# Hybrid decoder layer: FFN input normed ahead of its products, 18 of 22 up pairs by seven block products, gated products through DRAM, the down projection as one stage, w_out weights kept

## The chip, the cores and the metric

The kernel runs on one core of one Trainium2 chip. The metric is the device time of one execution in microseconds (us). Shorter is better. TensorE (PE) multiplies; VectorE (DVE), ScalarE (ACT) and GpSimd (POOL) work element by element; SyncE (SP) and the queues of ACT and POOL start the transfers between DRAM and the on-chip memory.

## The reference

One decoder layer over 1024 prompt tokens and 32 sample tokens (8 sequences of 4), all in fp32. Cut to the half of the layer that the change touches:

```
merged = sum_i sigmoid(g_i) * (y_i @ W_branch_i)      # three token mixers, y_i
x   = x + rmsnorm(merged @ w_out) * g_post
up  = (rmsnorm(x) * g_pre_f) @ w_up                    # 1024 -> 2 * 2816
upc = causal_dwconv3(up) + b                           # over time, 3 taps a channel
fa, fb = split(upc)                                    # 2816 each
x   = x + rmsnorm((silu(fa) * fb) @ w_down) * g_post_f # 2816 -> 1024
```

The layer also returns its states: among them the last rows of the key and value caches (`out_wk`, `out_wv`: for the sample tokens the old cache less its first 4 rows, so a copy from DRAM to DRAM, with the new rows filled in elsewhere) and the last two values of `up` of each channel (`out_fx`).

## The kernel before

**Products.** The 1056 tokens stand in three chunks of 352 columns. Activations and weights are held as a high and a low part of a 32-bit format that PE multiplies, and a product of two numbers is three matmuls: high by high, high by low, low by high. A weight piece is four blocks of 128 by 128; it is loaded on SP's queue (L133) and split by `split`: ACT copies out the high part (L89, `wh`), DVE subtracts to get the low part (L95, `wl`). A ring of three pieces lies between the splitting and PE; `make` asks for pieces some places ahead. `products` multiplies one output tile of 128 channels: with k = 1024 it takes 8 blocks times 3 matmuls times 3 chunks, 72 matmuls of 352 columns. An up pair is two such tiles, `za` and `zb` of the same j, and there are 22 pairs (`w_up` as 44 tiles).

**Seven block products.** The ten pairs of gate tiles earlier in the program go through `strassen` instead: the pair is taken as a 2 by 2 block matrix (two tiles by two halves of k), the input as 2 by 2 blocks (two halves of k by two column halves of 264), and seven products of blocks stand for eight. That is 168 matmuls of 264 columns a pair. It needs sums of input blocks, made once by `combos` into the buffer Y, sums of weight blocks (four DVE additions a pair on 128 by 512), and sums of results: some results are written by ACT to their place, and others are added by DVE from the accumulators "mm", "aux" and "wb".

**Stages.** After the start (the norm of x, then gates of the first chunk), the gates and the mixers, the branch products end at 640.13 us. Then `w_out` is multiplied in three passes, one a chunk, each of which loads and splits all its weights again (24 units of 24 matmuls). After a chunk's pass, `chain` brings it on while PE works on the next one: sum of squares by a product with ones, root (`rstd_of`, `factor_of`: DVE L295, the power on POOL L296, spread by four transposes L301), times the factor, plus x loaded from DRAM, the sum written to `x2d`, squares, and another root into R. `operands` makes the FFN input x times `g_pre_f` without that root (L903, L904), in Y; the root, which is one factor a token, is multiplied in when an up result leaves its accumulator (`evac_u`, by DVE). So up products start before the second root is known. The last chunk's chain (`last_chain`) runs beside the up pairs j = 0 and 1.

**Up and down.** Then the pairs j = 2 to 21: two units, the convolution over time (`conv`: ACT L983, then DVE L985 twice a tile), silu (L1036), the product, and its split into high and low parts in a ring of five slots, from which `down` takes groups of four as soon as they are there: DOWN lists after which j which k are multiplied. M holds the down sums of all chunks. The last group and the final norm follow.

**Order.** PE's instructions run in the order in which the code makes them; those of the other engines are put in order by a scheduler at build time, so a line may be moved far from where it is written. SP issues nearly all loads.

Of the kernel before, what the change touches and what calls it, by code (L numbers as in the profile page):

```python
# [31 lines left out]
RING = 5  # L32
LAST = 18
DOWN = {4: [(0, 4)], 8: [(4, 8)], 12: [(8, 12)], 16: [(12, 16)], 21: [(16, 18)]}
# [5 lines left out]
def body(tc, i, o):  # L40
# [3 lines left out]
    with top, tc.manual_schedule(engines={mybir.EngineType.PE}):  # L44
# [15 lines left out]
        M8 = M.rearrange("p (k t) -> p k t", k=8)  # L60
        x2d = dram.tile([P, 8, T], F32, name="x2d")

# [57 lines left out]
        xraw = [None]  # L120
# [25 lines left out]
        def make(ahead):  # L146
            while len(made) < min(ahead, len(items)):
                need, _, fn = items[len(made)]
                load(need + 4)
                if len(raws) <= need:  # L150
                    break
                made.append(fn())

        def add(src, nk, eng, where=None):
            for k0 in range(0, nk, 4):
                n = min(4, nk - k0)
                w = None if where is None else [t[:, k0 : k0 + n, :] for t in where]
# [3 lines left out]
                def fn(at=at, n=n, w=w):  # L161
                    raw, raws[at] = raws[at], None
                    return split(raw, n, w, eng)
# [3 lines left out]
        def add_pair(one, two):  # L167
# [7 lines left out]
            def part(q):  # L175
                def fn():
# [6 lines left out]
                    if q == 6:  # L183
                        tt(raws[at + 1], raws[at + 1], raws[at], ALU.subtract)
# [9 lines left out]
        def products(nk, hi, lo, evac, chunks=CHUNKS, cols=cc, pieces=None):  # L194
            ps = {}
            for pi, k0 in enumerate(range(0, nk, 4)):
# [6 lines left out]
                else:  # L203
                    make(pieces + pi + (3 if pieces >= lastw else 1))
# [44 lines left out]
        def combos(X, to, p):  # L249
# [4 lines left out]
            to4 = lambda n, h: to[:, ((p * 4 + n) * 2 + h) * 4 * HC :][:, : 4 * HC].rearrange("p (k t) -> p k t", k=4)  # L254

            def part(n, z):
                copy(to4(n, 0), z)
                sub(to4(n, 1), z, f32(to4(n, 0)))
# [47 lines left out]
        hs = ExitStack()  # L306
        with hs:
            hp = open_pool(hs, "hp", bufs=1)
            H = hp.tile([P, 16, T], F32R, name="H")
            Hhi, Hlo = (lambda k: H[:, k, :]), (lambda k: H[:, 8 + k, :])  # L310
            win = lambda u: i["win"][u]


            sigd = dram.tile([P, 24, T], F32, name="sigd")
            Yf = Y.rearrange("p s t -> p (s t)")

            nc.scalar.dma_start(cst[:, :NC1], i["cst"][:, :NC1])
            dve.memset(nhalf, -0.5)
            dve.memset(ones, 1.0)
            warm = fixed.tile([P, 4], F32, name="warm")  # L320
            copy(warm, nhalf)
            make_identity(nc, ident)
            for u in range(3):
                add(win(16 + u), 8, dve, [Y[:, 8 + 2 * u + h, 0:1024].rearrange("p (k m) -> p k m", k=8) for h in range(2)])
            add(win(19), 8, dve)
            for u in range(20, 40, 2):
                add_pair(win(u), win(u + 1))
            for u in (0, 1, 2):
                add(win(u), 8, dve)
            for u in range(3, 16):  # L330
                add(win(u), 8, pool)
            for n in range(8):
                add(i["wa"][n], 2, dve)
                add(i["wc"][n], 2, dve)
                add(i["wb"][n], 4, dve)
            for c in CHUNKS:
                for n in range(8):
                    add(i["wo"][n], 8, dve)
            for eng in (dve, pool):
                for j in range(2):  # L340
                    for part in range(2):
                        add(i["wu"][j + NFF * part], 8, eng)
            for j in range(2, NFF):
                for part in range(2):
                    add(i["wu"][j + NFF * part], 8, dve)
                for g0, g1 in DOWN.get(j, ()):
                    for n in range(8):
                        add(i["wd"][n, :, g0:g1, :], g1 - g0, dve)
            lastw = len(items)
            for n in range(8):  # L350
                add(i["wd"][n, :, LAST:NFF, :], NFF - LAST, pool if n % 2 else dve,
                    [Y[:, 2 + n, 512 * h : 512 * (h + 1)].rearrange("p (k m) -> p k m", k=4) for h in range(2)])
            room[3] = R[:, 544:T]

            def load_x(c, k, n=2):
                nc.sync.dma_start(M8[:, k : k + n, cc(c)], i["x"][c, :, k : k + n, :])

            load(1)
            load_x(0, 0, 1)
            load_x(0, 1, 1)  # L360
            for k in (2, 4, 6):
                load_x(0, k)
            load(4)
            for c in (1, 2):
                for k in range(0, 8, 2):
                    load_x(c, k)

            with ExitStack() as gs:
                psW = open_pool(gs, "psW", bufs=2, space=PSUM)
                banks[:] = [(psA, "mm")] * 3 + [(psW, "wb")] * 2  # L370
                sg = open_pool(gs, "sg", bufs=1)

                def evac_gate(u):
                    def f(c, ps):
                        s = sg.tile([P, CW], F32, name="g", bufs=3)
# [21 lines left out]
                def end(c):  # L397
                    later[c]()
                    normed(c)
# [844 lines left out]
```

## Time and profile before

| | |
|---|---|
| median of 3 runs | 1554.22 us (1553.83 to 1555.48) |
| the profiled run's own time | 1555.17 us |
| its span in the profile | 1553.5 us |
| start, until the first product of the gates | 0 to 44.0 us |
| gate pairs by seven block products | 84.8 to 289.5 us |
| mixers and branch products | to 640.1 us |
| `w_out`, and up pairs 0 and 1 | 640.1 to 807.7 us |
| up pairs 2 to 21 with the down groups | 807.7 to 1483.2 us |
| last down group and final norm | 1483.2 to 1553.5 us |

The lines of such a profile are read as follows. A row on a group of instructions has the line, the engine, the operation, the written and the read buffers, the shape and the count; behind the first bar the busy time of all in us and the mean of one in ns; behind the second the idle time of that engine just before them, and what ended it. The chain of waits goes back from the last instruction to what released each step, and each of its rows has a start, a duration and the instruction. The windows list for a stretch its length, the busy time (and number of instructions) of PE, PE's weight loads, DVE, ACT and POOL, then PE's granted clock (1.00 is full), the mean share of the 16 DMA engines that was busy, and GB/s. A busy share of DMA just above 1 is a rounding of the profile and means full.

### The profile page before, as it was taken

Reading aid. Unit: us, or ns where it says so; the run is one execution under the profiler, and the core shown is the slowest. Engines: PE = TensorE matmul, PEld = TensorE weight load, DVE = VectorE, ACT = ScalarE, POOL = GpSimd, SP = SyncE. Lnnn points to the kernel's source line nnn. Section 1 sums busy time; section 2 is a strip of 40 time slices with the busy share of each in tenths; the row PEclk is TensorE's granted clock in tenths of the full one; section 3 lists DMA queues with packets and bytes.
Section 4 is the critical chain, followed back from the end, with each engine's and each line's share of the span. In section 5 each row is a group of like instructions: output and inputs, shape, how many; then the busy total and the mean of one; then the engine's idle time right before and its main releaser. Section 6 shows DMA issues by size and latency. Waiting matters only on the chain.

```text
span 1553.5 us, 24657 instructions
## 1 busy us (share of the span) xinstructions
PE 1491.7 (96%) x9707; PEld 1479.0 (95%) x9707; DVE 875.1 (56%) x1542; ACT 583.7 (38%) x1123; POOL 317.5 (20%) x378
## 2 busy tenths in 40 slices
PE   5899999999999999978999999999999999999995
PEld 5899999998999899978999999999999999999995
DVE  7744445237676366577766515653654555355757
ACT  6344444356764322445442332321321232132343
POOL 2100000023553045244571101100110010010024
PEclk9999999999999999999999999999999999999997
DMA  6123332210002176444531111111111111111225
GB/s 221 52 97 111 106 109 84 82 50 28 28 22 77 46 232 189 135 149 156 175 99 48 48 42 48 48 42 48 48 42 48 48 41 49 48 41 45 65 73 175
DMA packets 77187, 128.01 MB, mean 82 GB/s; under 512 B 8192, under 2 KB 34752, under 8 KB 77056
## 3 DMA queue, kind: packets, MB, share of 16 engines
q1 hardware_dynamic: 68896, 111.66, 22.8%
q10 hardware_dynamic: 8032, 13.41, 2.3%
q8 instruction: 76, 1.25, 0.3%
q0 software_dynamic: 144, 1.38, 0.2%
q14 instruction: 39, 0.32, 0.1%
HBM read 104.17 MB, written 23.26 MB: 82 GB/s over the span
## 4 chain that ended last, share of the span: by engine, by line
PE 88%; DVE 6%; POOL 2%; ACT 2%; issue 1%; DMA 1%; SPq 0%; POOLq 0%; ACTq 0%; DVEq 0%
PE mm L98 54%; PE mb L98 23%; PE aux L98 6%; PE wb L98 3%; DVE M L92 2%; POOL rs L296 1%; PE sp L98 1%; ACT M L673 1%; DVE Y L904 1%; PE aux L686 1%; DVE M L390 0%; POOL R L92 0%; DVE M L667 0%; DMA M<-in_x 0%; DVE wl L95 0%
## 5 line engine op out<-in xcount | busy, mean ns | idle before, releaser
L98 PE MATMUL mm<-Y,wh 128*128 128x352 f32 (+1 forms) x1984 | 453.8, 314 | 0.0
L89 ACT ACTIVATE wh<-raw 128x512 fp32r<-128x512 f32 (+1 forms) x242 | 147.0, 608 | 522.8 <-PE mm L98 213.2
L98 PEld LDWEIGHTS mm<-Y,wh 128*128 128x128 f32 x1984 | 337.5, 189 | 0.0
L98 PE MATMUL mm<-Y,wl 128*128 128x352 f32 (+1 forms) x992 | 312.0, 315 | 0.7 <-DVE wl L95 0.7
L98 PE MATMUL mm<-H,wh 128*128 128x352 f32 (+1 forms) x1184 | 282.4, 323 | 1.6 <-DVE Y L95 0.9
L98 PE MATMUL mb<-Y,wh 128*128 128x352 f32 x992 | 241.8, 325 | 0.0
L95 DVE TENSOR_TENSOR wl<-raw,wh 128x512 fp32r<-128x512 f32 (+1 forms) x208 | 154.2, 741 | 144.8 <-ACT wh L89 144.3
L98 PEld LDWEIGHTS mm<-H,wh 128*128 128x128 f32 x1184 | 203.9, 191 | 2.5 <-PE aux L98 1.1
L98 PE MATMUL mm<-H,wl 128*128 128x352 f32 (+1 forms) x592 | 189.7, 320 | 4.1 <-DVE wl L95 4.0
L98 PEld LDWEIGHTS mm<-Y,wl 128*128 128x128 f32 x992 | 186.1, 188 | 1.0 <-DVE wl L95 1.0
L98 PEld LDWEIGHTS mb<-Y,wh 128*128 128x128 f32 x992 | 174.1, 189 | 0.0
L98 PE MATMUL mb<-Y,wl 128*128 128x352 f32 x496 | 161.4, 325 | 0.0
L985 DVE SCALAR_TENSOR_TENSOR cz<-U,cst,cz 128x1072 f32<-128x1072 f32 x88 | 118.2, 1344 | 31.6 <-ACT cz L983 30.3
L98 PE MATMUL mm<-ring,wh 128*128 128x352 f32 x524 | 126.6, 323 | 0.0
L980 POOL COPY fx<-U 128x2 f32<-128x2 f32 x44 | 30.2, 687 | 460.7 <-DVE U L92 460.7
L98 PEld LDWEIGHTS mm<-H,wl 128*128 128x128 f32 x592 | 112.9, 191 | 5.1 <-DVE wl L95 5.1
L95 DVE TENSOR_TENSOR wl<-xraw,wh 128x512 fp32r<-128x512 f32 x70 | 48.5, 692 | 90.0 <-ACT wh L89 89.5
L98 PEld LDWEIGHTS mb<-Y,wl 128*128 128x128 f32 x496 | 93.4, 188 | 0.0
L98 PEld LDWEIGHTS mm<-ring,wh 128*128 128x128 f32 x524 | 91.6, 188 | 0.0
L92 DVE TENSOR_TENSOR U<-mm,R 128x352 f32<-128x352 f32 (+2 forms) x106 | 43.1, 428 | 80.7 <-PE mm L98 80.7
L92 DVE TENSOR_TENSOR M<-mm,M 128x352 f32<-128x352 f32 (+3 forms) x95 | 47.4, 505 | 70.8 <-PE mm L98 70.5
L98 PE MATMUL mm<-ring,wl 128*128 128x352 f32 x262 | 84.7, 323 | 0.0
(228 smaller groups left out, 2336.6 us busy)
## 6 DMA issues: line engine op xcount, KB each, us to landing
raw<-in_wu SPq DMA_DIRECT2D x96, 256.0 KB, 2.6
sig<-sigd SPq DMA_DIRECT2D x72, 176.0 KB, 3.1
raw<-in_wo SPq DMA_DIRECT2D x48, 256.0 KB, 2.7
sigd<-M ACTq DMA_DIRECT2D x40, 264.0 KB, 2.1
xraw<-in_win SPq DMA_DIRECT2D x40, 256.0 KB, 2.6
raw<-in_wd SPq DMA_DIRECT2D x40, 256.0 KB, 2.6
raw<-in_win SPq DMA_DIRECT2D x39, 256.0 KB, 2.6
x2d<-M SPq DMA_DIRECT2D x12, 352.0 KB, 4.2
```

Source lines behind the costliest of these rows:

```text
L89: act.activation(out, in_, AF.Copy)
L92: return eng.tensor_tensor(out, a, b, op=op)
L95: eng.tensor_tensor(out, a, b, op=ALU.subtract)
L98: pe.matmul(out, lhsT, rhs, start=start, stop=stop, skip_group_check=more)
L296: pool.tensor_tensor(v, v, nhalf[:bs, :nb], op=ALU.pow)
L673: act.activation(s[:, h, :], s[:, h, :], AF.Exp, bias=ng[:, h : h + 1], scale=SCALE, accum_out=l[:, h : h + 1])
L686: pe.transpose(pt[:, h * P : (h + 1) * P], s[:, h, kb * P : (kb + 1) * P], ident)
L904: dve.scalar_tensor_tensor(l, x, g_pre_f[:, k : k + 1], f32(h), ALU.mult, ALU.subtract)
L980: pool.tensor_copy(fx[:, f, 0:2], u[:, 1024:1026])
L985: dve.scalar_tensor_tensor(z, u[:, s : s + CONV], cwf[:, f, s : s + 1], z, ALU.mult, ALU.add)
```

## The change

- **Input of the FFN.** `chain` now also multiplies x by `g_pre_f` and by the second root, in place in M, and splits the result into H (which lives to the end). All three chunks go this way, the last one beside up pairs 0 and 1. `evac_u` is now a plain copy by ACT. The additions of the chain move from POOL to DVE.
- **Up pairs.** j = 3 to 20 go through `strassen`, with `evac_up` for the results (`put` is a copy by ACT, or an addition by DVE where its last argument is true); j = 0, 1, 2 and 21 stay plain. `combos` builds the sums of input blocks in Y, one column half beside pairs 0 and 1 and one after them. The weight blocks of a pair are loaded into M. In a block pair's list of weight sums the fourth is made with the other three, at the third product.
- **Gated products.** `act_pair` writes the product of `za` and `zb` to DRAM (`y2d`, ACT's queue). `load_y` reads it back on SP's queue and splits it (ACT, then DVE) into slots of Y and H, during the last up pair and the down groups. `down` is one stage behind all up pairs: the same five groups and the last one.
- **Weights of w_out.** The 8 units are loaded and split once, at the first chunk, and kept in Y (and one tile); the up weights of j = 0 and 1 are kept too, for the three chunks. `limit` keeps `make` from writing a slot that is still read.
- **Queues.** The two cache copies, and the load of `sff`, are issued from ACT instead of POOL.

The core of the diff, without the shift of indentation that it brings:

```diff
-DOWN = {4: [(0, 4)], 8: [(4, 8)], 12: [(8, 12)], 16: [(12, 16)], 21: [(16, 18)]}
+DOWN = [(0, 4), (4, 8), (8, 12), (12, 16), (16, 18)]
+PLAIN = 3
...
+                        tt(raws[at + 1], raws[at + 1], a11, ALU.subtract)
-                    if q == 6:
-                        tt(raws[at + 1], raws[at + 1], raws[at], ALU.subtract)
...
+        for n in range(1, 8):
+            add(i["wo"][n], 8, dve, whole([Y[:, 2 * n + h, :] for h in range(2)]))
...
+            if PLAIN <= j < NFF - 1:
+                add_pair(i["wu"][j], i["wu"][j + NFF])
+                continue
...
-                                nc.gpsimd.dma_start(o["wk"], i["ck"][:, 4:, :])
-                                nc.gpsimd.dma_start(o["wv"], i["cv"][:, 4:, :])
+                            nc.scalar.dma_start(o["wk"], i["ck"][:, 4:, :])
+                            nc.scalar.dma_start(o["wv"], i["cv"][:, 4:, :])
...
                     tt(m, m, rs.unsqueeze(1).to_broadcast([P, 2, CW]), ALU.mult)
-                    tt(m, m, xs[n // 2], ALU.add, pool)
+                tt(m, m, xr[n // 2 % 2], ALU.add)
...
+            spread = rstd_of([acc2[:, 0, :], acc2[:, 1, :]], R[:, cc(c)])
             yield
+            spread()
+            yield
+            for n in range(0, 8, 2):
+                m = M8[:, n : n + 2, cc(c)]
+                for k in range(n, n + 2):
+                    x = M8[:, k, cc(c)]
+                    dve.scalar_tensor_tensor(x, x, g_pre_f[:, k : k + 1], R[:, cc(c)], ALU.mult, ALU.mult)
+                h, l = H[:, n : n + 2, cc(c)], H[:, 8 + n : 10 + n, cc(c)]
+                copy(h, m)
+                sub(l, m, f32(h))
...
             def evac_u(u):
-                        tt(u[:, 2 + c * CW : 2 + (c + 1) * CW], ps, R[:, cc(c)], ALU.mult)
+                        copy(u[:, 2 + c * CW : 2 + (c + 1) * CW], ps)
...
+            def evac_up(j):
...
+                def f(q, p, t):
+                    if q < 2:
+                        put(to(0, True, p), t, q)
+                    if q in (2, 6):
+                        put(to(0, False, p), t, q == 6)
+                    if q == 3:
+                        held[p] = t
+                    if q == 4:
+                        put(to(1, False, p), t, False)
+                        put(to(1, False, p), held[p], True)
+                    if q == 5:
+                        put(to(1, True, p), t, False)
+                return f
...
-                    copy(h, a)
-                    sub(l, a, f32(h))
+                nc.scalar.dma_start(y2d[:, j, :], za[:, :T])
...
+            for c in CHUNKS:
+                if c == 2:
+                    combos(M8, 0)
+                for j in range(2):
+                    for part in range(2):
+                        for _ in up_unit(j, part, (c,), pieces=upw + 4 * j + 2 * part):
+                            for step in steps[1:]:
+                                next(step, None)
+                    if c == 2:
+                        act_pair(j)
+            combos(M8, 1)
...
+            for j in range(PLAIN, NFF - 1):
+                for part in range(2):
+                    old(*tile_of(j, part))
+                for _ in strassen(B, new, evac_up(j)):
+                    pass
+                act_pair(j)
...
+            def load_y(k):
+                h, l = slots[k]
+                nc.sync.dma_start(f32(l), y2d[:, k, :])
+                copy(h, f32(l))
+                sub(l, f32(l), f32(h))
```

The order of instructions shows it at three places. The first is the head of ACT's list, at the very start of the program, before the change (`warm` is a first small activation, `Y<-raw` the copy of the first weight piece, `sq<-M` a square of the norm of x):

```order
L1227 UNCONDITIONAL_BRANCH
L317 DMA cst<-in_cst 128x80
L89 ACT_TABLE_LOAD
L89 ACTIVATE warm<-nhalf 128x4
L89 ACTIVATE Y<-raw 128x512
L407 ACTIVATE acc<-M 128x704
```

and with the change:

```order
L1274 UNCONDITIONAL_BRANCH
L319 DMA cst<-in_cst 128x80
L91 ACT_TABLE_LOAD
L91 ACTIVATE warm<-nhalf 128x4
L862 DMA out_wk<-in_ck 8x15872
L863 DMA out_wv<-in_cv 8x15872
L91 ACTIVATE Y<-raw 128x512
L418 ACTIVATE acc<-M 128x704
```

The two cache copies now stand with no wait among the first transfers of the program; before, they stood on POOL, behind twelve products of the branch stage.

The second place is DVE in the stretch from the last units of `w_out` to up pair 1, with the change (`R<-R,sq` adds squares of the third chunk; `M<-M 128x4x264` is a difference of input blocks in `combos` and `Y<-M,Y` the low part of one; `M<-M,cz` a factor or x, that lies in `cz`, on the third chunk; `M<-M 128x512` a sum of weight blocks for pair 3; L938 the new norm, `H<-M,H` a low part of the FFN input):

```order
L94 TENSOR_TENSOR R<-R,sq 128x352
L97 TENSOR_TENSOR Y<-M,Y 128x1056
L94 TENSOR_TENSOR M<-M 128x4x264
L97 TENSOR_TENSOR Y<-M,Y 128x1056
L300 TENSOR_SCALAR rs<-aux 88x4
L94 TENSOR_TENSOR M<-M 128x4x264
L97 TENSOR_TENSOR Y<-M,Y 128x1056 x2
L94 TENSOR_TENSOR M<-M,cz 128x2x352 x4
L94 TENSOR_TENSOR M<-M 128x512
```

Before the change POOL had the additions of that stretch:

```order
L92 TENSOR_TENSOR R<-R,sq 128x352
L92 TENSOR_TENSOR M<-M,xr 128x2x352 x2
L92 TENSOR_TENSOR R<-R,sq 128x352
L92 TENSOR_TENSOR M<-M,xr 128x2x352
L92 TENSOR_TENSOR acc_7802<-acc_7802,sq_7861 128x704
```

So the chain's additions and the block sums now share DVE, where the scheduler has put one half of `combos` ahead of the third chunk's chain.

The third place is DVE in one up pair by block products (`U` are the up results before the convolution, `cz` those behind it):

```order
L94 TENSOR_TENSOR M_78<-M_78 128x512 x2
L97 TENSOR_TENSOR wl_10498<-M_78,wh_10497 128x512
L94 TENSOR_TENSOR U0_7912<-aux_10406,U0_7912 128x264
L94 TENSOR_TENSOR M_78<-M_78 128x512
L94 TENSOR_TENSOR U0_7912<-aux_10419,U0_7912 128x264
L97 TENSOR_TENSOR wl_10551<-M_78,wh_10550 128x512
L1032 SCALAR_TENSOR_TENSOR cz_10529<-U0_7912,cst_71,cz_10529 128x1072
L1032 SCALAR_TENSOR_TENSOR cz_10535<-U1_7913,cst_71,cz_10535 128x1072
L1032 SCALAR_TENSOR_TENSOR cz_10529<-U0_7912,cst_71,cz_10529 128x1072
L97 TENSOR_TENSOR wl_10585<-M_78,wh_10584 128x512
L94 TENSOR_TENSOR U2_7914<-wb_10588,U2_7914 128x264
```

and DVE in one plain pair before the change:

```order
L92 TENSOR_TENSOR U_8106<-mm,R 128x8x4
L95 TENSOR_TENSOR wl<-raw,wh 128x512
L95 TENSOR_TENSOR ring<-cz,ring 128x1024
L95 TENSOR_TENSOR ring<-cz,ring 128x32
L985 SCALAR_TENSOR_TENSOR cz<-U_8106,cst,cz 128x1072 x2
L95 TENSOR_TENSOR wl<-raw,wh 128x512
L92 TENSOR_TENSOR U_8107<-mm,R 128x352 x2
```

So the rows of the convolution (L1032) of one pair now stand together, between those of the next pair's weight sums and results; before, they stood two by two behind a split of a gated product, with the evacuation of each chunk after them.

More of the change, by code (lines that the diff above doesn't have):

```diff
@@ new lines, in body @@
+        hp = open_pool(top, "hp", bufs=1)
+        H = hp.tile([P, 16, T], F32R, name="H")
+        Hhi, Hlo = (lambda k: H[:, k, :]), (lambda k: H[:, 8 + k, :])
+        win = lambda u: i["win"][u]
+        sigd = dram.tile([P, 24, T], F32, name="sigd")
+        nc.scalar.dma_start(cst[:, :NC1], i["cst"][:, :NC1])
+        dve.memset(nhalf, -0.5)
+        dve.memset(ones, 1.0)
+        warm = fixed.tile([P, 4], F32, name="warm")
+        copy(warm, nhalf)
+        make_identity(nc, ident)
+        for u in range(3):
+            add(win(16 + u), 8, dve, [Y[:, 8 + 2 * u + h, 0:1024].rearrange("p (k m) -> p k m", k=8) for h in range(2)])
@@ L937, in body @@
-            steps = []
-            for c in CHUNKS:
-                acc = pc.tile([P, 2, CW], F32, name="acc") if c < 2 else R[:, cc(2)]
-                for n in range(8):
-                    unit(8, Hhi, Hlo, evac_o(n, acc), (c,))
-                    for step in steps:
-                        next(step, None)
-                if c < 2:
-                    steps.append(chain(c, acc))
-            pcs.close()
-        rp = open_pool(top, "rp", bufs=1)
-        ring = rp.tile([P, 2 * RING, T], F32R, name="ring")
@@ new lines, in attend_sample @@
+                        copy(ph[:rows, : nb * P], pt[:rows, : nb * P])
+                        yield
+                        for b in range(nb):
+                            c0 = (4 * p + b) * P + 64 * g
+                            v = vc[:, c0 : c0 + 64] if p < 2 else vs[:, 64 * g : 64 * g + 64]
+                            mm(yo, v, ph[:rows, b * P : (b + 1) * P], p == 0 and b == 0, p == 2)
+                    y = room[h, 1024:1152].rearrange("p (j t) -> p j t", j=4)
+                    copy(y, yo.rearrange("p (j t) -> p j t", j=4))
@@ new lines, in body, with flow @@
+            copy(wth, wraw)
+            sub(wtl, wraw, f32(wth))
+            pool.affine_select(wss, wss, pattern=[[0, 4], [1, NS]],
+                               compare_op=ALU.is_ge, fill=0.0, base=0, channel_multiplier=-1)
+            def flow(*evacs):
+                for ev in evacs:
+                    if ev in halos:
+                        halo_a(halos[ev])
+                    yield from products(8, Hhi, Hlo, ev)
+            halos = {}
+            for _ in flow(evac_v, evac_cv(0), evac_k, evac_q(0), evac_q(1)):
+                pass
@@ new lines, in body @@
+        limit[0] = upw + 2
+        steps = []
+        for c in CHUNKS:
+            acc = pc.tile([P, 2, CW], F32, name="acc") if c < 2 else R[:, cc(2)]
+            for n in range(8):
+                unit(8, Hhi, Hlo, evac_o(n, acc), (c,), pieces=wow + 2 * n)
+                if c == 2 and n < 4:
+                    limit[0] = upw + 2 * n + 2 if n < 3 else 1 << 30
+                    make(min(limit[0], upw + 8))
+                for step in steps:
+                    next(step, None)
+            if c < 2:
+                pair = lambda name, **kw: pc.tile([P, 2, CW], F32, name=name, **kw)
+                steps.append(chain(c, acc, pc.tile([P, CW], F32, name="rs"), [pair("xr", bufs=2) for _ in range(2)],
+                                   pair("acc2"), pair("sq3")))
```

1238 lines of the change are left out of this document (597 added, 641 removed).

## The prediction

> **What bounds the kernel now.** I first read the page's busy shares and slices, then the shares of the chain of waits, then the windows by stage.
>
> ```profile
> PE 1491.7 (96%) x9707; PEld 1479.0 (95%) x9707; DVE 875.1 (56%) x1542; ACT 583.7 (38%) x1123; POOL 317.5 (20%) x378
> PE   5899999999999999978999999999999999999995
> PE 88%; DVE 6%; POOL 2%; ACT 2%; issue 1%; DMA 1%; SPq 0%; POOLq 0%; ACTq 0%; DVEq 0%
> 84.80:289.50 204.70, 204.70 (x1675) 204.70 (x1674) 95.29 (x166) 89.34 (x188) 1.15 (x3) 1.00 0.31 103
> 640.13:807.70 167.57, 150.02 (x912) 146.94 (x912) 110.45 (x133) 80.46 (x145) 79.85 (x64) 0.95 0.47 150
> 877.60:1483.20 605.60, 605.60 (x3747) 605.60 (x3746) 310.33 (x481) 159.32 (x222) 48.32 (x102) 1.00 0.16 49
> ```
>
> PE is 96% busy and 88% of the chain, and from 877.6 to 1483.2 us it does not stop. There only fewer matmul columns can shorten the time. The gaps are at the start, at the end and in the stretch of w_out (the 7 and 8 in the slices): there 17.55 of 167.57 us are idle, and the clock is 0.95. The gate pairs, which already go by seven block products, keep PE full too, with DVE busy for 95.29 of 204.70 us.
>
> **1. Block products for 18 pairs.** The chain shows the first products of two gate pairs in sequence, and a plain up tile:
>
> ```profile
> 153.43 5.84 PE mm L98 x48
> 173.88 5.84 PE mm L98 x48
> 854.57 11.65 PE mm L98 x72
> ```
>
> A block pair takes 173.88 − 153.43 = 20.45 us for its 168 matmuls (0.1217 each), a plain tile 11.65 for 72 (0.1618 each), so a plain pair 23.30. The saving is 2.85 a pair, 18 × 2.85 = **51.3 us**, if the up pairs keep that pitch. The gates had no convolution beside them, so I add up what the other engines hold in a pair:
>
> ```profile
> L985 DVE SCALAR_TENSOR_TENSOR cz<-U,cst,cz 128x1072 f32<-128x1072 f32 x88 | 118.2, 1344 | 31.6 <-ACT cz L983 30.3
> L92 DVE TENSOR_TENSOR cz<-cz 128x1024 f32<-128x1024 f32 x22 | 26.9, 1222 | 0.6
> L95 DVE TENSOR_TENSOR wl<-xraw,wh 128x512 fp32r<-128x512 f32 x70 | 48.5, 692 | 90.0 <-ACT wh L89 89.5
> L92 DVE TENSOR_TENSOR xraw<-xraw 128x512 f32<-128x512 f32 x40 | 27.5, 686 | 0.7
> L92 DVE TENSOR_TENSOR M<-aux,M 128x264 f32<-128x264 f32 x40 | 17.2, 429 | 7.5 <-PE aux L98 6.9 <-ACT M L89 0.6
> L983 ACT ACTIVATE cz<-U,cst 128x1072 f32<-128x1072 f32 x44 | 56.5, 1283 | 9.8 <-DVE U L92 9.8
> L1036 ACT ACTIVATE cz<-cz 128x1072 f32<-128x1072 f32 x22 | 24.2, 1099 | 52.7 <-DVE cz L985 52.7
> L89 ACT ACTIVATE wh<-xraw 128x512 fp32r<-128x512 f32 x70 | 44.1, 630 | 67.3 <-PE mm L98 23.4 <-PE aux L98 20.1 <-PE wb L98 19.9
> L89 ACT ACTIVATE M<-mm 128x264 f32<-128x264 f32 x60 | 22.9, 382 | 21.7 <-PE mm L98 21.7
> ```
>
> DVE has four rows of convolution, the gated product, seven low parts, four weight sums and six additions of results: 4 × 1.344 + 1.222 + 7 × 0.692 + 4 × 0.686 + 6 × 0.429 = 16.8 us of 20.45. ACT has 2 × 1.283 + 1.099 + 7 × 0.630 + 8 × 0.382 = 11.1. Both fit. Order can still make PE wait. A weight piece is asked for two block products ahead (2 × 24 × 0.1217 = 5.84 us), and its copy and low part take 1.32, so 4.5 us of other DVE rows may stand ahead of it: three convolution rows (4.03) do, as the order of after has them, four (5.38) would not. On ACT a result must leave the accumulator "mm" before the same column half is added to again, that is within the other half's 12 matmuls, 1.46 us: behind one convolution row the copy takes 1.283 + 0.382 = 1.67, which is 0.2 too late, where the two fall together. I take no wait; at 0.2 for each of two copies it would be 0.4 a pair, 7 us, which goes into the range.
>
> **2. The cache copies at the start.** They now stand among the first transfers.
>
> ```profile
> 6.16 6.49 DMA M<-in_x
> 44.02 9.35 PE wb L98 x48
> 10.00:12.00 2.00, 1.32 (x9) 1.32 (x10) 2.00 (x4) 1.67 (x4) 0.00 (x0) 1.00 1.07 397
> out_wk<-in_ck POOLq DMA_DIRECT2D x1, 496.0 KB, 5.2
> out_wv<-in_cv POOLq DMA_DIRECT2D x1, 496.0 KB, 7.2
> 568.17 0.75 POOL L848 DMA_DIRECT2D out_wk<-in_ck  x1
> 568.92 0.53 POOL L849 DMA_DIRECT2D out_wv<-in_cv  x1
> ```
>
> The chain begins with a load of x that lands at 12.65 and leads without a gap to the first product of the gates at 44.02. The 16 DMA engines are full (1.07 and 397 GB/s between 10 and 12 us), so what comes between pushes x back. Where the copies ran before, the first landed at 568.17 + 5.2 = 573.4 and the second at 568.92 + 7.2 = 576.1, so 2.7 us each once started, 5.5 together. Bounds: 0 (if they yield to the loads) and 7.2; by volume, 0.99 MB at 397 GB/s, 2.5. I take 5.3, near the time that they needed themselves, as they are issued ahead of most of x.
>
> The Trainium skill ("DMA: Bandwidth & Descriptors", How many engines) says that the slowest dimension of a transfer sets how many of the 16 engines it uses. The copies' is 8, so 8 engines would carry them while x needs all 16. By that rule 2.7 us each is half the rate, and x waits for the loaded half: 5.5 rather than 2.5. No row here shows the engines one by one; the 2.7 agrees with it.
>
> **3. w_out to up pair 1.** PE's own work there is 36 units of 24 matmuls, 36 × 24 × 0.1618 = 139.8 us, and six roots.
>
> ```profile
> 710.37 0.55 PE aux L98 x8
> 714.84 0.30 PE aux L301 x4
> PE mb L98 <- DVE wl L95: 10.2, 4, 5.5
> 694.00:696.00 2.00, 1.68 (x6) 0.50 0.29 95
> 696.00:698.00 2.00, 2.00 (x8) 0.50 0.79 242
> 698.00:700.00 2.00, 2.00 (x10) 0.63 0.77 235
> ```
>
> Six roots at 0.85 make 144.9 before; with three of the sums in two parts, as the change has them, 3 × 0.55 more, 146.5. So 22.7 us are lost now: 17.55 idle, and some 5 at a lower clock. After the long wait (5.5) the clock is 0.50 to 0.63, and 24 matmuls take 5.68 us where they need 3.88: 1.8 lost. The waits for `wl` go, as the weights are kept. What is late next is the chain, whose every step I laid by these rows:
>
> ```profile
> L92 DVE TENSOR_TENSOR M<-M,rs 128x704 f32<-128x704 f32 x8 | 13.1, 1696 | 0.9 <-ACT rs L89 0.9
> L92 DVE TENSOR_TENSOR M<-M,cz 128x704 f32<-128x704 f32 x4 | 3.3, 884 | 0.3 <-ACT cz L89 0.3
> L92 DVE TENSOR_TENSOR M<-M 128x1056 f32<-128x1056 f32 x8 | 10.0, 1252 | 0.0
> 22.22 7.22 POOL rs L296
> 12.73 0.80 ACT sq L407
> cz<-in_x SPq DMA_DIRECT2D x4, 352.0 KB, 4.3
> ```
>
> Five waits follow, where PE's list has the sums or transposes that need the chain. **Chunk 0:** after the factor is spread (8.9 us into the second pass) come four steps of 1.70 + 0.88, three additions of squares at 0.88 and a last square, 0.8: 22.6 us, and PE is there after five units and 0.85, at 20.2; 2.4. **Chunk 1:** the same in the third pass, where DVE also splits up weights and adds squares of chunk 2, four times 0.69 and five times 0.43 (by the addition of 264 columns above); a third of these 4.9 falls on the chain; 4.1. **Chunk 2, first sum:** the last addition of squares stands behind a block sum and its low part (1.25 + 0.9); 2.1. **Its transposes:** the power on POOL takes up to 7.22 where DVE streams beside it, and the row ahead of it on DVE 1.25, against the unit of 3.88 in between; 4.6. **Its second sum:** two x loads wait for their buffers, 4.3 each; factor and addition of the first step (2.6) and a second (2.6), x landing at 9.9, addition, square, two half additions (0.9 + 0.8 + 0.9), a copy of the factor (0.4), a weight sum (0.7) make 13.6, against three half units, 5.8: 7.8. Together 21.0 us, and three of them are long, at 1.7 of slow clock each (the 1.8 above, a little less for the shorter ones) 5.1. 146.5 + 21.0 + 5.1 = 172.6, that is **+5.0** against 167.57. What queues behind a wait is PE's own list, so each of them moves the end. Bounds: with no wait 146.5, −21; with DVE's whole block sums (8 × 1.25) ahead of the chain another 7, +12.
>
> The Trainium skill ("TensorE: Matmul & The Clock Gate", Part 1) says that the clock halves after an idle window of about 3.4 us and comes back after as long of work. The rows agree: 0.50 behind 5.5 us. By it the waits of 2.4 and 2.1 cost no clock and the slow clock adds 5.1; if every wait cost as much as that one, it would be 8.5.
>
> **4. The down stage, `y2d` and what else moves: 0.** The matmuls of the down groups are the same in number and columns. A gated product is stored and read back at least one group before its use.
>
> ```profile
> sigd<-M ACTq DMA_DIRECT2D x40, 264.0 KB, 2.1
> sig<-sigd SPq DMA_DIRECT2D x72, 176.0 KB, 3.1
> ```
>
> A round trip like that takes 5.2 us, and a group of four lasts 8 × 4 × 9 × 0.1618 = 46.6. DMA is at 0.16 in that stage, and SP has only the weights in its queue ahead. If a slot came late, one trip would show: 0 to +6. The additions that leave POOL are in part 3, and the evacuations that go from DVE to ACT in part 1.
>
> **Sum.** −51.3 + 5.3 + 5.0 + 0 = −41.0. The profiled run took 1555.17 us (span 1553.5 and 1.7 around it), 0.95 above the median. So 1514.2 by the run and 1513.2 by the median; with part of the 0.2 us copies I say **1515.0**.
>
> **Rivals.**
> - *Copies cost nothing, and the chain is no later than before.* Speaks for it: the chain loses its detours over POOL, and part 3 is the part with most steps that no row shows in their new order. 1554.2 − 51.3 = 1502.9.
> - *Accumulator copies wait on ACT* behind convolution and silu rows: 1.283 + 1.099 + 0.382 − 1.46 = 1.3 us once a pair, 18 × 1.3 = 23 more: 1538. Against it: ACT is free for 9 of 20.45 us.
> - *DVE becomes the bound (slower).* If the scheduler's rows put the four convolution rows ahead of a weight piece, that piece is 5.38 − 4.5 = 0.9 late; if this befalls three of the seven pieces, 2.7 a pair, 49 us: 1564. It decides from 41.0 / 18 = 2.3 us a pair on. Against it: 16.8 of 20.45 us leave 3.6 free, and the order of after has pieces between the third row and the fourth.
> - *The block products don't pay here* (264 columns bring no gain): the gate pairs speak against it; 1515 + 51 = 1566.
>
> **How the numbers follow.** Forecast (1506 to 1527) 0.60; first rival 0.19; ACT's waits 0.13; slower by DVE 0.05; no gain 0.03. The range 1500 to 1532 takes the forecast, the first rival and the lesser half of the ACT case. A measurement here tells some 0.2% (3 us) from no change: faster 0.92, same 0.02, slower 0.06.
>
> **What would show it.** In the profile of after: rows of the chain 20.45 us apart in the up pairs, with PE at 100% (else a wait "PE mm <- ACT U", or "<- DVE wl", names the rival); the first product of the gates at about 49 rather than 44 us, with the x load landing near 18; from the first product of w_out to up pair 2 about 173 us, with the waits above, the longest on squares of chunk 2; a full PE in the down groups. I am wrong if the pairs lie at 21.5 us or more, or if the start has not moved.

## The result, and the profile after

The changed kernel takes 1514.16 us (median of 4 runs, 1513.63 to 1515.21) against 1554.13 before (1553.83 to 1555.48). The ratio is 0.9742 with a 95% interval of 0.9725 to 0.9759: 2.6% faster. The forecast was 1515.0. The span of its profile is 1511.9 us against 1553.5, that is 41.6 less.

The head of the page of the changed kernel: busy times and shares, PE's slices, the shares of the chain of waits.

```profile
PE 1442.8 (95%) x10163; PEld 1431.5 (95%) x10163; DVE 913.3 (60%) x1611; ACT 658.6 (44%) x1338; POOL 271.0 (18%) x333
PE   4899999999999999999879999999999999999995
PE 89%; DVE 5%; ACT 2%; POOL 1%; DMA 1%; issue 1%; SPq 0%; ACTq 0%; DVEq 0%
```

PE is still the bound, busy for 49 us less, and the chain is still PE for 89%. Where the stages begin is read from the chain of waits of the changed kernel (start, duration, what; xN is a number of matmuls):

```profile
47.48 9.34 PE wb L100 x48
643.60 7.78 PE wb L100 x48
820.29 3.82 PE wb L100 x24
843.21 2.95 PE mm L100 x24
854.91 5.84 PE mm L100 x48
875.36 5.84 PE mm L100 x48
1442.37 6.56 PE mm L100 x36
```

These are the first product of the gates, of w_out, of up pair 2 and of the block pairs, two block pairs one after the other, and the last down group. Against the rows of before:

| stretch | before | after | difference |
|---|---|---|---|
| to the first product of the gates | 44.02 | 47.48 | +3.46 |
| gates, mixers, branch products, to w_out | 596.11 | 596.12 | 0 |
| w_out and up pairs 0 and 1 | 167.8 | 176.7 | +8.9 |
| up pairs 2 to 21 and the down groups | 675.2 | 622.1 | −53.2 |
| last down group and norm | 70.3 | 69.5 | −0.8 |

(Pair 2 of before stands at 807.95 in the chain, a quarter of a microsecond behind the boundary taken in the prediction.) So 12.3 us were lost ahead of pair 2, and 53.2 gained behind it. In the stretch of the 18 block pairs the windows of the changed kernel show no idle PE at all (length, busy time of PE, PEld, DVE, ACT and POOL, clock, DMA):

```profile
843.21:1211.27 368.06, 368.06 (x3026) 368.06 (x3026) 277.52 (x427) 186.91 (x362) 72.93 (x108) 1.00 0.23 80
```

368.06 / 18 = 20.45 us a pair, the pitch of the gates. DVE takes 277.52 / 18 = 15.4 us and ACT 10.4 of a pair, where 16.8 and 11.1 had been added up: the convolution found its place.

The other side is the stretch from w_out to pair 2. PE's waits there in the changed kernel (who waited for whom: us in total, times, the longest):

```profile
PE aux L100 <- DVE acc L94: 7.8, 2, 5.2
PE aux L100 <- issue: 5.6, 1, 5.6
PE aux L306 <- POOL rs L301: 5.6, 1, 5.6
PE aux L100 <- DVE R L94: 2.0, 1, 2.0
```

The five waits in PE's timeline of the same kernel (start, duration, instruction; in square brackets the wait before it and what ended it):

```profile
693.84 2.51 PE L100 MATMUL aux<-ones,acc 128*88 128x1 f32 x16 [2.60 <-DVE acc L94]
735.84 2.47 PE L100 MATMUL aux<-ones,acc 128*88 128x1 f32 x16 [5.23 <-DVE acc L94]
755.68 0.76 PE L100 MATMUL aux<-ones,R 128*88 128x1 f32 x8 [1.98 <-DVE R L94]
764.03 0.85 PE L306 MATMUL aux<-ident,rs 88*128 88x88 f32 x4 [5.55 <-POOL rs L301]
777.99 2.60 PE L100 MATMUL aux<-ones,cz 128*88 128x1 f32 x16 [5.58 <-issue]
```

Every wait is a sum or a transpose of the chain that stands in PE's list before its input is there. Together 20.9 us. The windows of PE show what comes on top (length, busy time with the number of matmuls, then the clock):

```profile
690.00:694.00 4.00, 1.40 (x9) 0.92 0.96 316
694.00:698.00 4.00, 4.00 (x22) 0.50 0.12 46
736.00:740.00 4.00, 4.00 (x22) 0.50 0.46 153
764.00:768.00 4.00, 3.97 (x16) 0.50 0.55 194
780.00:784.00 4.00, 4.00 (x17) 0.50 0.01 2
```

Around four of the five waits, the one of 2.60 us too, the clock falls to half and stays there for some microseconds of work. The first of these windows shows that it falls during the wait: a mean of 0.92 over 4 us is 0.6 us at half clock, so from 693.4 us on, and PE's sum begins only at 693.84.

### The profile page after: what moved, and what is told of

The parts are those of the page before. It is cut to its first block, busy times and chain, and to the rows that moved or that the text cites. A ratio compares the mean times of both kernels' runs of the same rounds, so it can differ in the third digit from the quotient of the medians.

```text
span 1511.9 us, 25762 instructions
## 1 busy us (share of the span) xinstructions
PE 1442.8 (95%) x10163; PEld 1431.5 (95%) x10163; DVE 913.3 (60%) x1611; ACT 658.6 (44%) x1338; POOL 271.0 (18%) x333
## 4 chain that ended last, share of the span: by engine, by line
PE 89%; DVE 5%; ACT 2%; POOL 1%; DMA 1%; issue 1%; SPq 0%; ACTq 0%; DVEq 0%
PE mm L100 53%; PE wb L100 20%; PE aux L100 13%; DVE M L94 2%; POOL rs L301 1%; PE sp L100 1%; ACT M L684 1%; DMA M<-in_x 1%; PE aux L697 1%; DVE M L678 0%; DVE eacc L94 0%; DMA raw<-in_wu 0%; PE aux L306 0%; DVE Y L97 0%; DVE H L97 0%
## 5 line engine op out<-in xcount | busy, mean ns | idle before, releaser
L100 PE MATMUL mm<-Y,wh 128*128 128x264 f32 (+1 forms) x1880 | 377.7, 296 | 0.0
L100 PE MATMUL mm<-Y,wl 128*128 128x264 f32 (+1 forms) x940 | 277.8, 296 | 0.0
L91 ACT ACTIVATE wh<-raw 128x512 fp32r<-128x512 f32 (+1 forms) x106 | 61.6, 581 | 204.0 <-PE mm L100 130.6
L100 PE MATMUL wb<-H,wh 128*128 128x264 f32 (+1 forms) x720 | 147.6, 298 | 0.0
L1032 DVE SCALAR_TENSOR_TENSOR cz<-U,cst,cz 128x1072 f32<-128x1072 f32 x88 | 114.0, 1330 | 12.6 <-ACT cz L1030 12.4
L100 PEld LDWEIGHTS wb<-H,wh 128*128 128x128 f32 x720 | 116.3, 188 | 0.0
L100 PE MATMUL mm<-H,Y 128*128 128x352 f32 x624 | 110.8, 338 | 2.6 <-DVE H L97 2.6
L97 DVE TENSOR_TENSOR wl<-M,wh 128x512 fp32r<-128x512 f32 x126 | 86.4, 686 | 41.2 <-ACT wh L91 41.2
L100 PEld LDWEIGHTS mm<-H,Y 128*128 128x128 f32 x624 | 107.2, 199 | 3.0 <-DVE H L97 3.0
L100 PE MATMUL wb<-H,wl 128*128 128x264 f32 (+1 forms) x360 | 107.2, 298 | 0.0
L97 DVE TENSOR_TENSOR wl<-raw,wh 128x512 fp32r<-128x512 f32 (+1 forms) x80 | 56.1, 701 | 52.0 <-ACT wh L91 52.0
L94 DVE TENSOR_TENSOR M<-M 128x512 f32<-128x512 f32 (+1 forms) x88 | 69.5, 789 | 26.8 <-DMA M<-in_wu 25.9
```

The lines of the kernel that those rows point to most:

```text
L91: act.activation(out, in_, AF.Copy)
L94: return eng.tensor_tensor(out, a, b, op=op)
L97: eng.tensor_tensor(out, a, b, op=ALU.subtract)
L100: pe.matmul(out, lhsT, rhs, start=start, stop=stop, skip_group_check=more)
L1032: dve.scalar_tensor_tensor(z, u[:, s : s + CONV], cwf[:, f, s : s + 1], z, ALU.mult, ALU.add)
```

## Experiments

All times are medians; each ratio is to runs of the kernel before that were taken together with it, 1553.5 to 1554.6 us in the median. In the table the stretch is from the sum of squares of w_out's first chunk to the first product of up pair 2, read from PE's timeline and the chain. "Waits" is PE's idle time in it. "Clock" is what the lowered clock cost there: busy time times (1 − clock), added up over windows of 0.2 us. What is left of the stretch is 112.1 us before and 112.6 to 113.4 in all the others, so these two terms account for the differences.

| kernel | time | ratio to before (95%) | stretch | waits | clock |
|---|---|---|---|---|---|
| before | 1554.13 | | 137.0 | 17.5 | 7.4 |
| changed kernel | 1514.16 | 0.9742 (0.9725 to 0.9759) | 145.8 | 20.9 | 11.9 |
| e1 copies late | 1510.25 | 0.9720 (0.9706 to 0.9735) | 146.0 | 21.4 | 11.7 |
| e2 all pairs plain | 1557.03 | 1.0016 (1.0000 to 1.0032) | 145.3 | 20.2 | 12.2 |
| e3 state late | 1514.56 | 0.9746 (0.9731 to 0.9762) | 145.8 | 18.4 | 14.8 |
| e4 sums of the chain later | 1502.79 | 0.9668 (0.9651 to 0.9685) | 134.4 | 14.6 | 6.9 |
| e5 pair 2 by block products | 1513.76 | 0.9744 (0.9722 to 0.9766) | | | |
| e6 gated products loaded twice | 1514.91 | 0.9742 (0.9715 to 0.9770) | | | |
| e7 before, copies early | 1556.12 | 1.0021 (1.0002 to 1.0040) | | | |
| e8 four together | 1481.81 | 0.9538 (0.9517 to 0.9558) | 121.6 | 5.1 | 3.4 |
| e9 as e8, block sums early | 1497.51 | 0.9650 (0.9614 to 0.9685) | 129.8 | 12.1 | 4.5 |
| e11 as e8, tuned | 1486.37 | 0.9578 (0.9548 to 0.9609) | 120.3 | 3.5 | 3.4 |
| e12 as e11, pair 2 too | 1496.37 | 0.9630 (0.9590 to 0.9669) | | | |

### The cache copies: e1 and e7

e1 issues them from POOL as before; e7 is the kernel before with the opposite edit.

```diff
-                            nc.scalar.dma_start(o["wk"], i["ck"][:, 4:, :])
-                            nc.scalar.dma_start(o["wv"], i["cv"][:, 4:, :])
+                            nc.gpsimd.dma_start(o["wk"], i["ck"][:, 4:, :])
+                            nc.gpsimd.dma_start(o["wv"], i["cv"][:, 4:, :])
```

> The changed kernel with the two cache copies issued from POOL behind the branch products, as they were. Theory (the copies among the first loads push x back): the first product of the gates returns from 47.48 to about 44.0 us and the time falls by 3.5, to about 1510.7. Rival (the start moved because the other first loads changed their order): the first product stays near 47.5 us and the time at 1514.

> The kernel before, with one part of the change alone: the two cache copies issued from ACT, where they land at the start. Theory (the copies push the first loads of x back by 3 to 4 us): 1557 to 1558. Rival (something else in the start of the changed kernel): 1554, no change.

The chain at the start of the changed kernel: the second and third power of the first norms on POOL (the first product of the gates, at 47.48, is shown above).

```profile
26.28 7.22 POOL rs L301
41.58 5.34 POOL rs L301
```

The same rows of e1, with the product of the gates:

```profile
22.59 7.22 POOL rs L301
37.88 5.94 POOL rs L301
44.71 10.16 PE wb L100 x48
```

And those of e7:

```profile
26.34 7.22 POOL rs L296
41.63 2.40 POOL rs L296
44.59 7.82 PE wb L98 x48
```

With the copies at the start, both powers begin at 26.3 and 41.6 us, in either kernel; with the copies late at 22.6 and 37.9 (22.2 and 37.5 before the change). So the copies cost 3.7 to 4.1 us, and the rivals, another order of the first loads or something else in the start, fall: the one edit alone moves the start of either kernel. The other profiles agree: the second power begins at 22.2 to 23.4 us in the six with the copies late and at 26.2 to 27.9 in the eight with the copies at the start. ACT's first work on x shows the delay at its source, before and with the change:

```profile
5.38 0.79 ACT L407 ACTIVATE acc<-M 128x704 f32<-128x704 f32 x1 [0.41 <-DMA M<-in_x]
10.02 0.79 ACT L418 ACTIVATE acc<-M 128x704 f32<-128x704 f32 x1 [5.48 <-DMA M<-in_x]
```

The first loads of x come 4.6 us later. How the copies hold them up isn't shown: their issues have no time of landing in the profile, and its windows there give DMA shares that can't be right (2.15 from 3 to 4 us, 0.20 from 4 to 5).

The third power itself took 2.40 us in e7 and 5.94 before, which gave the loss back in that profile; the time of e7 lies between theory and rival, 0.2% longer than before, with an interval from 0.02 to 0.4%. e1 is 3.9 us faster than the changed kernel, all of its runs (1509.52 to 1511.94) below all of that kernel's, though the two intervals of the ratios meet; the two profiles differ by 1.7, as e1's is of its slowest run.

### The block products: e2

```diff
-PLAIN = 3
+PLAIN = 21
```

> The changed kernel with all 22 up pairs plain (PLAIN = 21); sums of input blocks are still made, nothing else differs. Theory: 18 pairs at 23.3 or (with the operand in H, as up pair 2 shows) 22.9 us in place of 20.45, so 44 to 51 us more, 1558 to 1566. Rival (a good part of the gain comes from something else, such as kept weights or the norm ahead of the products): 30 us more or less, under 1545.

42.9 us more, just under the theory's lower end, and level with the kernel before. The plain pairs in the chain of e2:

```profile
861.22 3.82 PE wb L100 x24
865.04 11.45 PE mm L100 x72
```

A plain tile takes 11.45 us here, not 11.65: 0.1590 a matmul, so 22.9 a pair, and 18 × (22.9 − 20.45) = 44. Block products thus bring some 44 of the 51 us against the pairs of before. The other 7 are a faster plain pair, which the changed kernel would have without them: its operand lies in H, where it lay in Y (why that matters is open, see e10). In its profile e2 loses 11.3 us ahead of pair 2 and gains 9.7 from there on, so that without block products the change is no faster than before.

### The waits from w_out to pair 2: e3, e4, e8, e9, e11

e3 puts the first four copies of the conv state `sff` into U behind the powers on POOL:

```diff
-                if 0 in chunks:
-                    old(f, u)
+                if chunks == (2,):
+                    with tc.issue_after(root[0].ins):
+                        old(f, u)
+                elif 0 in chunks and len(chunks) > 1:
+                    old(f, u)
```

> The changed kernel with the four first copies from sff into U put behind both powers of the last chunk on POOL. Theory (the power waits in POOL's queue behind copies that wait for the transfer of sff): the wait of PE for POOL's power falls from 5.55 to about 1.6 us, and the time by 4 to 6. Rival (the power is starved while DVE streams, as the prediction had it): the power itself takes several us, the wait stays above 4, and the time within 1 us of 1514.

POOL's timeline in the changed kernel:

```profile
755.64 0.25 POOL L973 MEMSET U<- 128x2 f32 x4 [16.05 <-DVE R L94]
760.22 2.79 POOL L983 COPY U<-sff 128x16 f32<-128x16 f32 x4 [4.33 <-DMA sff<-in_sff]
762.97 1.01 POOL L301 TENSOR_TENSOR rs<-rs,nhalf 88x4 f32<-88x4 f32 x1
```

And in e3:

```profile
759.84 0.25 POOL L975 MEMSET U<- 128x2 f32 x4 [17.42 <-DVE R L94]
763.39 3.13 POOL L303 TENSOR_TENSOR rs<-rs,nhalf 88x4 f32<-88x4 f32 x1 [3.29 <-DVE rs L302]
```

In the changed kernel the power takes 1.01 us and no idle time stands before it: it was queued behind four copies that waited for a transfer. The prediction's cause of this wait (a starved power) is refuted for it. With the queue cleared the power comes as soon as its input is there, but takes 3.13 us beside a busy DVE, so the rival was not empty. From PE's sum to the end of the power it is now 6.64 us, where it was 8.30. PE's wait falls from 5.55 to 2.38, half of it because PE itself is slower there: the 12 matmuls ahead of the wait take 3.70 us at half clock, and took 2.19. The time does not fall (1514.56, stretch 145.8), which refutes the theory's 4 to 6 us: the waits are 2.5 us less in all and the lowered clock costs 2.9 more, 34.1 us of the stretch at half clock where it was 30.7.

e4 moves PE's sums and transposes down its list, and nothing else (the three gaps are 0, 2, 0 for chunks 0 and 1, and 1, 3, 1 for chunk 2):

```diff
+                for _ in range(gaps[0]):
+                    yield
                 spread()
...
+            for _ in range(gaps[1]):
+                yield
             spread = rstd_of([acc2[:, 0, :], acc2[:, 1, :]], R[:, cc(c)])
             yield
+            for _ in range(gaps[2]):
+                yield
             spread()
```

> The changed kernel with PE's sums and transposes of the chain put later in its list: two units later for the second sums of chunks 0 and 1; for chunk 2 the first transposes one half unit later, the second sum three more, the second transposes one more. Theory (PE only waits because it stands there too early, the chain has time until up chunk 2): most of the 15.4 us of waits for DVE and of the 9 us of lower clock behind the waits go, 12 to 24 less, 1490 to 1502. Rival (the chain of chunk 2 is the bound): the wait comes back at the first product of up chunk 2 as a wait for H, and the time falls by under 6.

11.4 us less, a little under the theory's 12; by the table 6.3 of them are waits and 5.0 the clock. PE's waits in this stretch of e4:

```profile
PE aux L100 <- issue: 7.7, 1, 7.7
PE aux L306 <- POOL rs L301: 4.6, 1, 4.6
PE aux L100 <- DVE acc L94: 2.2, 1, 2.2
```

The second sums of chunks 0 and 1 wait no more (7.8 us gone), and those units run at full clock, but chunk 2's second sum now waits 7.7 us, and chunk 1's first sum 2.2. That is half of the rival: the chain of chunk 2 does bind, though at its second sum and not at up chunk 2. That chain holds DVE rows of the block sums in between, and its power still stands behind the copies. So e8 takes e1, e3 and e4 together, with gaps of 1, 4 and 0 for chunk 2, and puts the block sums behind the chain (`end` is the last low part of chunk 2's norm on DVE):

```diff
-                if c == 2:
-                    combos(M8, 0)
...
-            combos(M8, 1)
+            with tc.issue_after(end[0].ins):
+                combos(M8, 0)
+                combos(M8, 1)
```

> The changed kernel with four things together: copies late as in e1, state copies behind the powers as in e3, PE's sums later as in e4 (two units for chunks 0 and 1; a half unit ahead of the first transposes of chunk 2 and four ahead of its second sum), and both column halves of the block sums behind the norm of chunk 2 on DVE. Theory (the waits from w_out to up pair 1 were places in PE's list and rows ahead of the chain on DVE and POOL): of the 20.9 us of waits at most 5 stay, the clock stays full, 1482 to 1492. Rival (the chain of chunk 2 takes longer than the PE work beside it): PE waits some 8 to 12 us for H at up chunk 2 or for its second sum, 1493 to 1500.

> The kernel of e8 less one part: the block sums of the first column half stay where the scheduler puts them, ahead of and among the chain of chunk 2 on DVE. Theory (some 10 us of block sums stand ahead of the chain, and PE waits for that chain): 8 to 15 us longer than e8, 1490 to 1497, with a wait of 5 us or more at the second sum of chunk 2 or at up chunk 2. Rival (the place of PE's sums alone made the gain): within 2 us of 1482.

e8 takes 1481.81 us: 32 us faster than the changed kernel and 4.6% faster than before. PE's waits in this stretch of e8:

```profile
PE aux L308 <- POOL rs L303: 2.9, 1, 2.9
PE aux L100 <- DVE acc L94: 2.2, 1, 2.2
```

And those of e9, which is e8 with the block sums where the scheduler had them:

```profile
PE aux L100 <- issue: 5.8, 1, 5.8
PE aux L308 <- POOL rs L303: 4.0, 1, 4.0
PE aux L100 <- DVE acc L94: 2.2, 1, 2.2
```

20.9 us of waits have become 5.1, and the stretch is 24.2 shorter: 15.8 by the waits and 8.5 by the clock, which cost 3.4 us rather than 11.9. So the theory has its time and its waits, but the clock did not stay full. e8's two waits show that the length of a wait does not decide what the clock does (columns as in the block pairs, the clock the third number from the end):

```profile
703.00:707.00 4.00, 3.42 (x16) 3.46 (x17) 3.71 (x6) 0.99 (x2) 0.21 (x1) 0.58 0.00 0
742.00:746.00 4.00, 1.15 (x8) 0.86 (x6) 3.10 (x4) 1.08 (x2) 3.98 (x1) 1.00 0.10 39
```

The wait of 2.2 us ends at 703.6, and the clock is at half from 703.7 to 710.5; the longer one, 2.9 us up to 746.0, leaves it at 1.00, and so does the wait of 2.2 us ahead of the same sum in e4 and e9.

The block sums' place is worth 8.2 us of the stretch (129.8 against 121.6), with e9's wait at the second sum as its theory had it; the time, 15.7 us above e8's, is a little over the theory's 15, and the rival falls. The profiles of e9 and e8 are 14.5 us apart (1495.2 and 1480.7 us): another 4.9 lie ahead of the stretch, where e8 had a short third power at the start (2.40 us, as in e7) and e9 one of 5.34 with a lower clock behind it, and 1.4 behind it. So some 3 us of e8's gain are that power, whose duration no edit here set on purpose. DVE's rows beside it, in e8 and in the changed kernel, show where it comes from:

```profile
40.43 0.69 DVE L97 TENSOR_TENSOR wl<-xraw,wh 128x512 fp32r<-128x512 f32 x1 [0.20 <-ACT wh L91]
43.02 0.68 DVE L97 TENSOR_TENSOR wl<-xraw,wh 128x512 fp32r<-128x512 f32 x1
```

In e8 DVE stood idle for 0.20 us from 40.23 on, waiting for ACT, and the power, begun at 38.71, ended 0.87 us after that; e7 has such a gap too. In the changed kernel DVE went on without a break until 46.03, and the power ended 0.88 us after that.

e11 shifts two places once more (chunk 0's second sum one unit later than in the changed kernel rather than two; chunk 2's gaps 2, 3 and 0):

> The kernel of e8 with PE's places tuned once more: the second sum of chunk 0 one unit later than in the changed kernel rather than two (so the norm of chunk 0 on DVE is done before the first root of chunk 1), and the first transposes of chunk 2 one more half unit later, its second sum at the same place. Theory: the two waits left in e8 (2.2 for the squares of chunk 1, 2.9 for POOL) go, 4 to 6 us less, 1476 to 1478. Rival (the chain needs that time anyhow and the wait moves to the second sum): 1480 to 1482.

The waits that e8 had left fall from 5.1 to 3.5, and the stretch by 1.3 us, but the time is 4.6 longer than e8's. Between the two profiles (3.0 us) 2.9 stand ahead of the stretch, where e11's third power took 5.94, and 1.4 behind it. Neither theory nor rival fits: the stretch gained a quarter of what was hoped, and the time missed both ranges.

### Pair 2 by block products: e5 and e12

`PLAIN = 2` in the changed kernel (e5) and in e11 (e12).

> The changed kernel with up pair 2 by block products too (PLAIN = 2). Theory (pair 2 is plain because the sums of input blocks are made on DVE meanwhile, some 20 us of its rows): PE waits 5 us or more for the second column half, and the time is 3 or more us longer, about 1517 or more. Rival (the sums are ready in time): 22.9 - 20.45 = 2.5 us less, 1511.7.

> The kernel of e11 with up pair 2 by block products too. Theory (the weight blocks of pair 2 are loaded over M, which the late block sums still read): PE waits, 3 us or more longer than e11. Rival: 2.5 us less than e11.

e5 refutes its theory: PE does not wait at pair 2, the block sums were there in time. The time is 0.4 us less, which is no difference that can be told, and not the rival's 2.5 either. In its profile the last down group ends 2.7 us earlier than in the changed kernel, 2.4 of them by pair 2; the final norm gives 1.3 back, where 12 matmuls took 2.50 us rather than 1.53. In e12 PE does wait at pair 2:

```profile
805.32 0.81 PE L100 MATMUL mm<-Y,wh 128*128 128x264 f32 x2 [7.81 <-ACT wh L91]
```

ACT, whose copy of the weights ended that wait, had itself waited for a convolution row of DVE shortly before:

```profile
801.32 1.10 ACT L1052 ACTIVATE cz<-cz 128x1072 f32<-128x1072 f32 x1 [5.89 <-DVE cz L1043]
```

On DVE these convolution rows stand among the late block sums, and the blocks are loaded over M, which the sums still read. So the theory has its wait, but whether the load or DVE's order made it isn't separated. The median is 10 us above e11's; one of its four runs (1487.95) is only 1.6 above, the other three 10 to 11. The early block sums had a use, for a kernel with pair 2 among the block pairs.

### The round trip through DRAM: e6

```diff
                 nc.sync.dma_start(f32(l), y2d[:, k, :])
+                nc.sync.dma_start(f32(l), y2d[:, k, :])
```

> The changed kernel with every gated product loaded twice from y2d (the second load overwrites the first with the same data). Theory (the round trip through DRAM lies beside full matmuls, term 4 of the prediction is 0): within 1.5 us of 1514. Rival (the loads are on the path, for instance by DMA time that the weights of down need): 22 loads of about 6.5 us each on SP's queue show, 10 us more at least.

1514.91 us: 22 more loads of 528 KB cost nothing that can be told, as the theory had it. The round trip is hidden.

### The pitch of a plain matmul: e10

> The changed kernel with 32 bytes of padding behind M, which moves the weight ring and H by 32 bytes and leaves Y where it is. Theory (352 columns take 0.1592 us with the operand in H and 0.1618 in Y because H lies at 32 modulo 64 bytes and Y at 0): up pair 2 goes from 0.1592 to 0.1618 a matmul. Rival (something else tells H from Y): it stays at 0.1592.

In the chain of e10, up pair 2 (operand in H), and a down unit with its operand in Y:

```profile
818.94 3.81 PE wb L101 x24
1253.37 5.77 PE mm L101 x36
```

H keeps 0.159 a matmul, so the theory falls. The groups in Y went from 5.83 to 5.77 for 36, although Y itself did not move. One run of 1512.31 us says nothing on the time.

## Why the prediction was right, point by point

1. **Block products, −51.3.** Right in its pitch: 20.45 us a pair, no wait on ACT or DVE in 368 us, so neither the 0.2 us of late copies nor the two rivals came. As a sum against before it holds (18 × 2.85); as a cause it is some 44 (e2), and 7 belong to a plain pair that is faster with its operand in H, which the prediction took for the same as in Y.
2. **Copies, +5.3.** Right in mechanism, too large: 3.5 in the first product, 3.7 to 4.1 at the powers (e1, e7). It lies between 2.5 (an even share of the bytes) and 5.5 (half of the engines, by the Trainium skill, "DMA: Bandwidth & Descriptors", How many engines), and no row tells which engines carried them. The sign that the prediction named, a load of x that lands near 18 us, did not come: the chain now begins with the first loads of x, at work from 10.02 us rather than 5.38, and goes on through the first norm.
3. **w_out to pair 1, +5.0.** It was +8.9, and the term of the sum that was mis-sized is the slow clock. The waits were forecast as 2.4, 4.1, 2.1, 4.6 and 7.8, and were 2.60, 5.23, 1.98, 5.55 and 5.58, together 20.9 against 21.0; that the single errors cancel is luck.

   The clock was put at 5.1, three long waits at 1.7, and cost 11.9. PE's own work was put at 146.5 and is 176.7 − 20.9 − 11.9 = 143.9, which hid a part of it. The 1.7 came from a misreading: the three windows with 6, 8 and 10 matmuls do not hold 24, since a window also counts a matmul that only reaches into it (at full clock a window of 2 us lists 14 or 15, and 2.00 / 0.1618 is 12.4). By the clocks of the same rows, 0.50, 0.50 and 0.63, some 2.6 us were lost, not 1.8.

   And the wait of 2.60 was followed by half clock as well: PE's sum of ones behind it took 2.51 us, against 1.34 in the same place in e4. For that the prediction had read the Trainium skill ("TensorE: Matmul & The Clock Gate", Part 1), an idle window of some 3.4 us, as if a shorter wait cost no clock. The trace disagrees with this reading: the clock fell 2.15 us into that wait, before the light products with ones began, and e8's waits of 2.2 and 2.9 us show that the place of a wait counts. e8 shows the size from the other side: with 15.8 us fewer waits the stretch fell by 24.2.
4. **The fourth wait** had its size nearly right for a wrong reason: copies ahead in POOL's queue, not a starved power (e3). Both exist; what the queue hid, 3.13 us of power in e3 and 4.00 in e8, came out when it was cleared.
5. **Down stage and `y2d`, 0.** Right: e6. The rest of that stage, with pairs 2 and 21 and two down groups in H, gained some 2 us that were not in the sum.

That the sum (−41.0 against −41.6) is nearer than its terms is luck: the clock was put 6.8 us too low, and against that stand 1.8 too much at the start, 2.6 too much in PE's own work from w_out to pair 2, and the 2 to 3 us of the end.

## What to carry to other kernels

When a stage is taken off PE's path, look where PE's own list asks for the results of a side chain: here five sums and transposes stood 2 to 6 us too early, and shifting them, with POOL's queue cleared and the block sums behind the chain, shortened the stretch by 24 us with no instruction less, a third of it by the clock alone. Count the clock as a term of its own, from windows, not as a fixed surcharge on long waits. Put a long side job that fills idle time behind the chain that someone waits for, and read the in-order queue ahead of a late instruction before blaming the instruction. An edit that changes only which queue issues a transfer may let a scheduler move it to the start, among the loads that everything waits for.

## What the runs showed of the hardware that was not expected

- A matmul of 128 by 352 took 0.1618 us with its moving operand in Y and 0.1592 in H, with weights from the ring; with weights kept in Y and the operand in H it took 0.1621 (7.78 us for 48). The 264-column ones took 0.1217 in both. In one profile 32 bytes of padding did not slow H, and sped up Y to 0.1603; the cause is open.
- From w_out to pair 2 the clock changed only on a fixed grid. It fell at 693.4, 734.4, 761.7 and 775.3 us in the changed kernel, 12, 20 and 24 times 3.41 us after the first, and at 692.7, 730.2 and 784.8 in the kernel before, 11 and 27 times. Each spell at half clock in the table's profiles lasted one, two or three times 3.41 us. So a wait of some 2 us costs nothing or up to 3.4 us of work, by where it falls: 2.15 us of idle time just ahead of such a moment were enough at 693.4, and 1.85 were not at 711.8 in e4 (that moment counted back in steps of 3.41 from the fall at 752.8). An edit that moves a wait can change the clock without changing the wait.
- The power on POOL over 88 by 4 values took 1.01 us while DVE was idle, and up to 7.22 while it was busy. Of 46 powers that took over 1.1 us at the start and from w_out to pair 2, over all profiles, 36 ended 0.86 to 0.89 us after the first idle moment in DVE's rows; eight of the other ten are the first power of kernels with early copies, of some 1.7 us. The same instruction at the start was 2.40 in two kernels, where DVE had a gap of some 0.2 us beside it, and 5.34 or 5.94 in others, which moves the whole program by 3 us.
